# Summing neighbours' features: pass 1 quad by quad with ReLU ranks, and ten instead of eight destination blocks by row gathers

## The chip, the cores and the metric

The kernel runs on one core of a Trainium2 chip. In it PE (TensorE) does the matmuls, DVE (VectorE) the comparisons, sums and products, ACT (ScalarE) copies and the ReLU, POOL (GpSimd) issues the gathers, and SP (SyncE) issues ordinary transfers; SBUF is the on-chip memory, and PSUM the one that PE writes to. In the profiles an instruction is named by the tiles that it writes and reads (psa, pso and psg are tiles in PSUM). The metric is the device time of one execution in microseconds (us). Every time of a run is a median of several executions unless said otherwise, with the range where it matters. A profile is one further reading of such an execution: its span is the time from the first to the last recorded instruction.

The recorded comparison and six further jobs gave two kinds of times, and this document depends on keeping them apart. The same kernel before takes about 395 us on chips 12, 1 and 3 and about 483 us on chips 0, 2 and 13. I call them the **quick** and the **late** kind, and for short speak of quick and late chips. Each chip was met in one job only, so whether the kind belongs to the chip or to the occasion is not shown; within a job it never changed. The recorded comparison fell on the late kind. The state that each run carries ("fast", or "slow" when it is over 1.5% above the fastest of its kernel) compares runs of one job and doesn't show this. Where slow runs would shift a difference, the fast ones alone are taken, and the text says so.

## The reference

```python
def reference(node_features, edge_index_src, edge_index_dst):   # 4096 x 128 f32; 65536 edges
    output = np.zeros((num_nodes, dim), dtype=np.float32)
    for i in range(len(edge_index_src)):
        output[edge_index_dst[i]] += node_features[edge_index_src[i]]
    return output
```

## The kernel before

The 4096 destinations are 32 blocks of 128. Three parts matter.

**Pass 1** sorts edges by destination block. The edges lie in 24 chunks, handled as six quads of four; each edge needs its rank among the edges of its block, and then a one-hot of the rank moves it to its place by a matmul. Before, the ranks came from one-hots of the block number for half the edges at a time, running sums on DVE for the first half, running sums on PE for the second, and a product on DVE that picks each edge's own count.

**Gathered blocks.** For the first KG blocks, POOL fetches the source rows of 128 edges with one gather (three bf16 parts of x, 768 bytes a row), and PE adds them up with a one-hot of the destination. That is 24 gathers and 24 sums per block.

```python
    def gather(d, q):                                  # one unit: 4 gathers
        t = xg.tile([P, 4, 3 * P], BF16, name="rows", tag="xg")          # GB = 6 buffers
        for l in range(4):
            G.indirect_dma_start(out=t[:, l, :], out_offset=None, in_=x3d[:, :],
                in_offset=bass.IndirectOffsetOnAxis(ap=gidx[:, place(q).start + l, d:d + 1], axis=0))
        rows[d, q] = t
    def gather_sum(d, q):                              # one unit: 4 sums, rows -> psg
        oh = sb2.tile([P, 4, P], BF16, name="ohg", bufs=6)
        onehot(oh[:], gkey[:, place(q), d, :], 4)
        ...
        for l in range(4):
            PE.matmul(out=psg[d][:, :3 * P], lhsT=oh[:, l, :], rhs=t[:, l, :], ...)
```

**Dense blocks.** The others, in GROUPS, get a second ranking (pass 2), and then a slot each: PE makes the 4096x128 matrix of edge counts (`psa`, copied to `a` by ACT) and multiplies it with x (`pso`).

```python
    def blocks(k, oh, a):                              # 8 times per slot
        psa = ps.tile([P, 512], F32, name="psa", tag="psA", bufs=3)
        for i in range(4):
            PE.matmul(out=psa[:, i * P:(i + 1) * P], lhsT=oh[0][:, k*4+i, :], rhs=oh[1][:, k*4+i, :], ...)
        S.copy(out=a[:, k * 4:k * 4 + 4, :], in_=psa[:]...)
    def product(k, a, pso):
        for s in range(k * 4, k * 4 + 4):
            PE.matmul(out=pso[:, :3 * P], lhsT=a[:, s, :], rhs=x3[:, s, :, :]..., ...)
```

## Time and profile before

| | us |
|---|---|
| timed, recorded job (the 3 runs known to the prediction) | 485.02 (482.05 to 487.04) |
| span of the profile given | 395.4 |
| pass 1 ends (last move matmul) | 100.3 |
| first copy of a dense block | 141.2 |
| from there to the end of the last product | 243.9 |

### The profile page before, as it was taken

How to read it: one execution, taken by the hardware profiler on the slowest of the kernel's cores; microseconds unless marked ns; L12 is line 12 of the kernel's file. 1: busy time of each engine (PE TensorE's matmuls, PEld its weight loads, DVE VectorE, ACT ScalarE, POOL GpSimd, SP SyncE). 2: the span in 40 equal slices, each digit the busy share in tenths (PEclk: the TensorE clock that was granted, in tenths of full speed). 3: DMA queues.
4: the chain of work that ended last, by engine and by line, in shares of the span. 5: the costliest groups of instructions: out<-in, count | busy, mean ns of one | idle time of the engine just before them, and what ended most of it. 6: DMA issues, size and time to landing. Idle time of an engine off the chain costs nothing.

```text
span 395.4 us, 7887 instructions
## 1 busy us (share of the span) xinstructions
PE 315.8 (80%) x3274; PEld 229.8 (58%) x3274; DVE 303.5 (77%) x532; ACT 146.1 (37%) x271; POOL 226.8 (57%) x216
## 2 busy tenths in 40 slices
PE   0598765797544679676996999999979999999990
PEld 0255664775442567454674777676747776666650
DVE  4998899899899962838799797678898957676310
ACT  2485400100000044132543445455545455546520
POOL 5832038877812777733588777565785775673000
PEclk9999865676675698896998999999999999999995
DMA  8999732232200233321022333232332332332000
GB/s 245 188 162 158 219 120 70 61 81 70 56 17 12 59 82 81 95 57 48 26 57 76 76 86 87 68 80 69 83 78 68 87 92 68 86 87 66 8 14 10
DMA packets 31014, 32.14 MB, mean 81 GB/s; under 512 B 3904, under 2 KB 27648, under 8 KB 30976
## 3 DMA queue, kind: packets, MB, share of 16 engines
q0 software_dynamic: 17536, 23.08, 27.3%
q1 hardware_dynamic: 13296, 8.01, 7.0%
q8 instruction: 26, 0.43, 0.4%
q10 hardware_dynamic: 144, 0.52, 0.4%
q14 instruction: 12, 0.10, 0.1%
HBM read 22.02 MB, written 5.39 MB: 69 GB/s over the span
## 4 chain that ended last, share of the span: by engine, by line
PE 54%; DVE 39%; issue 3%; DMA 1%; ACT 1%; DVEq 0%
PE pso L495 29%; PE psa L489 10%; DVE p L258 9%; PE psg L313 7%; DVE oh L258 6%; DVE v L226 4%; PE ps L462 4%; DVE cum L430 3%; DVE oh L411 3%; DVE oh L153 3%; PE psr L239 2%; DVE cum L357 2%; PE psr L438 2%; DVE v L424 2%; DVE cum L236 2%
## 5 line engine op out<-in xcount | busy, mean ns | idle before, releaser
L299 POOL DMA_INDIRECT rows<-x3d,gidx x192 | 207.3, 1080 | 119.8 <-issue 71.4
L495 PE MATMUL pso<-x,a 128*128 128x384 bf16 x768 | 160.7, 335 | 0.1
L491 ACT CAST a<-psa 128x512 bf16<-128x512 f32 x192 | 111.7, 588 | 109.5 <-PE psa L489 108.6
L489 PE MATMUL psa<-oh 128*128 128x128 bf16 x768 | 76.1, 223 | 13.9 <-DVE oh L258 13.0
L495 PEld LDWEIGHTS <-a 128*128 128x128 bf16 x768 | 69.3, 100 | 28.0 <-issue 3.0
L489 PEld LDWEIGHTS <-oh 128*128 128x128 bf16 x768 | 59.9, 100 | 40.8 <-DVE oh L258 14.4
L258 DVE TENSOR_TENSOR oh<-psi,slo 128x4096 bf16<-128x4096 uint16 x24 | 54.7, 2278 | 0.0
L258 DVE TENSOR_TENSOR oh<-psi,dlo 128x4096 bf16<-128x4096 uint16 x24 | 54.7, 2277 | 0.0
L313 PE MATMUL psg<-rows,ohg 128*128 128x384 bf16 x192 | 41.2, 359 | 14.4 <-DVE ohg L258 13.1
L321 DVE TENSOR_REDUCE res<-pso 128x128 f32<-128x384 f32 x24 | 13.3, 553 | 40.5 <-PE pso L495 40.5
L271 PE MATMUL psm<-v,p 128*128 128x64 bf16 x512 | 34.1, 239 | 10.4 <-DVE p L258 8.8
L258 DVE TENSOR_TENSOR p<-psi,rank 128x2816 bf16<-128x2816 uint16 x24 | 37.5, 1614 | 3.7 <-ACT rank L243 3.7
L271 PEld LDWEIGHTS <-p 128*128 128x128 bf16 x512 | 30.8, 121 | 14.1 <-DVE p L258 13.3
L313 PEld LDWEIGHTS <-ohg 128*128 128x128 bf16 x192 | 19.2, 106 | 28.7 <-DVE ohg L258 14.0
L258 DVE TENSOR_TENSOR p2b<-psi,rank 128x768 bf16<-128x768 uint16 x48 | 23.3, 547 | 14.2 <-PE ps L462 7.4
L176 POOL DMA_DIRECT2D xf<-x x8 | 14.7, 2278 | 13.6 <-ACT x L174 12.2
L462 PEld LDWEIGHTS <-p2b 128*128 128x128 bf16 x576 | 20.0, 102 | 1.8 <-issue 0.3
L258 DVE TENSOR_TENSOR ohg<-psi,gkey 128x512 bf16<-128x512 uint16 x48 | 18.2, 412 | 0.0
L277 ACT CAST sa<-psm 128x128 bf16<-128x128 f32 x6 | 1.6, 266 | 43.4 <-PE psm L271 43.4
L462 PE MATMUL ps<-v,p2b 128*128 128x32 bf16 x480 | 16.9, 197 | 0.0
L174 ACT ACTIVATE x<-xf 128x1024 bf16<-128x1024 f32 x12 | 12.4, 1055 | 7.5 <-DMA xf<-in_node_features_dram 7.5
L411 DVE TENSOR_SCALAR oh<-sbk 128x96 bf16<-128x96 bf16 (+1 forms) x128 | 14.0, 209 | 1.3 <-ACT sbk L278 1.3
(78 smaller groups left out, 234.6 us busy)
## 6 DMA issues: line engine op xcount, KB each, us to landing
xf<-x POOLq DMA_DIRECT2D x8, 512.0 KB, 8.9
x3d<-x SPq DMA_DIRECT2D x4, 768.0 KB, 8.7
rows<-x3d,gidx POOLq DMA_INDIRECT x192, 2.9
xf<-in_node_features_dram SPq DMA_DIRECT2D x4, 512.0 KB, 7.5
out_dram<-res SPq DMA_DIRECT2D x32, 64.0 KB, 1.8
raw<-in_edge_index_src_dram ACTq DMA_DIRECT2D x1, 512.0 KB
raw<-in_edge_index_dst_dram SPq DMA_DIRECT2D x1, 512.0 KB, 5.1
x3d<-zrow SPq DMA_DIRECT2D x1, 96.0 KB, 5.7
```

The lines of the kernel that those rows point to most:

```text
L176: G.dma_start(out=xf[i][:], in_=part, accum_op=OP.add)
L226: V.tensor_tensor(out=v1[q][:, :, k], in0=oh1[q // QH][:, :, q % QH], in1=key[:, q, :, None, :].to_broadcast([P, NJ, NB, 4]), op=OP.mult)
L258: V.tensor_tensor(out=dst.rearrange("p i (m k) -> p i m k", k=2), in0=io.rearrange("p i (m k) -> p i m k", k=2), in1=keys2[:, :, None, :]. ...
L271: PE.matmul(out=psm[:, l * 64:(l + 1) * 64], lhsT=p1[:, l % 2, j, :], rhs=v1[q][:, j, :, :, l].rearrange("p k b -> p (k b)"), start=j == j ...
L299: G.indirect_dma_start(out=t[:, l, :], out_offset=None, in_=x3d[:, :], in_offset=bass.IndirectOffsetOnAxis(ap=gidx[:, place(q).start + l, ...
L313: PE.matmul(out=psg[d][:, :3 * P], lhsT=oh[:, l, :], rhs=t[:, l, :], start=q == 0 and l == 0, stop=q == NQ - 1 and l == 3)
L321: V.tensor_reduce(out=res[:], in_=pso[:, :3 * P].rearrange("p (v f) -> p f v", v=3), op=OP.add, axis=AX.X, negate=True)
L411: V.tensor_single_scalar(out=oh2[:, :, :, s, :], in_=sbk[:, :, ds].rearrange("p c (i k) -> p c i k", k=4), scalar=float(s + 1), op=OP.is_e ...
L462: PE.matmul(out=ps2[:, d % per * NB:(d % per + 1) * NB], lhsT=p2b[d % 2][:, c, :], rhs=v2[:, c, d // 4, :, d % 4], start=c == 0, stop=c == ...
L489: PE.matmul(out=psa[:, i * P:(i + 1) * P], lhsT=oh[0][:, s, :], rhs=oh[1][:, s, :], start=True, stop=True)
L491: S.copy(out=a[:, k * 4:k * 4 + 4, :], in_=psa[:].rearrange("p (s m) -> p s m", s=4))
L495: PE.matmul(out=pso[:, :3 * P], lhsT=a[:, s, :], rhs=x3[:, s, :, :].rearrange("p v f -> p (v f)"), start=s == 0, stop=s == NB - 1)
```

## The change

The intent: make pass 1 cheaper on DVE (six quads one after another, one wide one-hot each, ranks from PE and a ReLU that subtracts 4096 instead of a product), and take two of 24 dense slots off PE by gathering their rows instead. The core of the diff:

```diff
-KG = 8
-GROUPS = (4, 8, 8, 4)
+BIG = 4096.0
+KG = 10
+GROUPS = (4, 8, 8, 2)
...
-    def oh1s(h):
-        for b in range(NB):
-            V.tensor_single_scalar(... scalar=float(b), op=OP.is_equal)
+    def oh1s(q):
+        onehot(oh1q(q), kd[q][:], NL, NB)
+        for j in range(NJ):                      # column sums of each chunk quad
+            PE.matmul(out=pst[:, j:j + 1], lhsT=oh1q(q)[...], rhs=ones[:, :1], start=True, stop=True)
+    def scan(q):
+        V.tensor_tensor_scan(out=sums[q][:], data0=ones[:, :NJ], data1=pst[:, :NJ], ...)
...
-    for j in range(1, NJ):
-        V.tensor_tensor(out=c[:, j], in0=c[:, j - 1], in1=o[:, j - 1], op=OP.add)
-            V.tensor_tensor(out=cum1[h][:, js], in0=cum1[h][:, js], in1=oh1[h][:, js], op=OP.mult)
+    def counts(q):
+        for j0 in range(0, NJ, 4):
+            PE.matmul(out=psc[:, :n * P], lhsT=early[:], rhs=oh1q(q)[...], ...)   # adds BIG at own place
+            for j in range(max(j0, 1), j0 + n):
+                PE.matmul(out=psc[...], lhsT=sums[q][:, j - 1:j].to_broadcast([P, P]), rhs=identb[:], ...)
+            S.activation(out=cum[...], func=RELU, bias=minus[:], in_=psc[:, :n * P]...)
...
     def pass2(g):
-        g4 = gd // 4
+        kk = 4 if gd % 4 == 0 else 2             # lets the last group have two blocks
...
+    for q in range(NQ):
+        move1(q, during(q))                      # counts of quad q + 2 and parts of x in between
```

The x parts are now issued between the ReLUs; from the second group on nothing changes but the last group of two and the longer list of gathers.

## The prediction

> **What bounds the kernel now.** I read the engine shares first, then the chain that ended last, then the groups, and last the order-of-time view of single engines, because the shares alone hide that this program has three stages with different limits.
>
> ```profile
> PE 315.8 (80%) x3274; PEld 229.8 (58%) x3274; DVE 303.5 (77%) x532; ACT 146.1 (37%) x271; POOL 226.8 (57%) x216
> ...
> PE   0598765797544679676996999999979999999990
> ...
> POOL 5832038877812777733588777565785775673000
> PEclk9999865676675698896998999999999999999995
> ```
>
> PE looks like the bound and POOL like an engine with 43% to spare. The slices correct the second impression: POOL's work starts only in the sixth slice (one slice is 9.9 us) and stops at 361 us; in between it is at seven to eight tenths. PE is full only from about 190 us on.
>
> Stage one (0 to 100 us, keys and pass 1) belongs to DVE: in the chain of waits it is a row of DVE one-hots (p, 1.53 us each), spreads (v, two of 1.53), running sums (cum, 21 of 0.37) and products (cum, 2.3). Stage two (101 to 146 us) prepares the first dense group, DVE and PE by turns. Stage three is 24 dense slots, one destination block each, and belongs to PE:
>
> ```profile
> 379.88 5.21 PE pso L495 x32
> ```
> ```profile
> L299 POOL DMA_INDIRECT rows<-x3d,gidx x192 | 207.3, 1080 | 119.8 <-issue 71.4 <-PE psg L313 42.6 <-PE psa L489 4.3
> L495 PE MATMUL pso<-x,a 128*128 128x384 bf16 x768 | 160.7, 335 | 0.1
> ...
> L313 PE MATMUL psg<-rows,ohg 128*128 128x384 bf16 x192 | 41.2, 359 | 14.4 <-DVE ohg L258 13.1
> ```
>
> The first line is the chain's last long piece (start, length): the last dense product, with nothing to hide behind. The groups give busy time and mean, then the idle time before and its releaser. For the gathers (L299) "issue 71.4" matters: 0.30 us that POOL needs between two gathers, beside the 0.95 us of one. POOL waited for somebody else only 42.6 us, for buffers that PE had not yet summed. In order of time (start, length, idle before):
>
> ```profile
> 126.70 3.89 POOL L299 DMA_INDIRECT rows<-x3d,gidx  x1 [0.30 <-issue]
> 130.90 0.95 POOL L299 DMA_INDIRECT rows<-x3d,gidx  x1 [0.31 <-issue]
> 132.15 0.95 POOL L299 DMA_INDIRECT rows<-x3d,gidx  x1 [0.30 <-issue]
> ```
>
> So the gather rhythm is 1.248 us (130.90 to 132.15) even when nothing is in its way, and some gathers take up to 4.6 us: the one at 126.70 lies beside a DVE product of two SBUF operands that ran from 126.43 to 129.77. POOL's true occupation is 192 x 1.248 = 240 us, plus about 23 us of stretched gathers (the excess over 0.95 added up), plus 43 us of waits: 306 us, which is 55.5 to 361. **It is an engine with 43 us to spare, not 170.**
>
> **What the Trainium skill says.** "SBUF — State Buffer", section "Who interferes with whom": a DVE instruction with two SBUF inputs contends with a GpSimd instruction that reads SBUF, and the second to issue blocks fully. The trace agrees: the 3.89 us above, 4.58 at 200.6 (beside the spread of the third group), 4.08 at 214.6 (beside its product), while one-hots whose first operand lies in PSUM leave gathers at 0.95. "TensorE: Matmul & The Clock Gate", Part 1: an idle array drops to half clock and a sustained busy window of about 3.4 us restores it. The trace agrees: granted clock 0.50 to 0.8 in most 3 us windows of pass 1, 1.00 from 220 us. "ScalarE: Activation LUTs", section "What ACT_TABLE_LOAD costs": a pointer operand as bias adds about 93 ns; no run yet shows it here, it concerns the new ReLU. "Runtime: NRT & Kernel Launch", section "Model-switch cost" (some 70 us on the first execution after another program) with its launch sequence of some 15 us: I take from it, as an estimate, that the 89.6 us between the timed 485.02 and the span of 395.4 is a constant that both kernels pay. If it were proportional, the result would move by less than 2 us.
>
> **The change part by part.**
> Pass 1, DVE. Gone: 21 running sums (7.5 us), four products (9.2 us), 64 comparisons (10.9 us). New: six one-hots of 2816 elements, at the 1.53 us rhythm of p, 9.2 us; six scans and six key shifts of 0.2 to 0.3 us, about 3 us; four more fmax reductions, about 1 us. Kept: 12 spreads and 24 one-hots. DVE loses about 14 us of work. In addition the first quad need no longer wait for half the edges.
> Pass 1, PE and ACT. Per quad PE gets 22 one-column sums, six 512-column counts, 21 small additions and 32 rank matmuls; by 0.064 to 0.11 us each at half clock, and 0.43 for a wide one, that is about 8.5 us beside the 6.0 us of the move itself (88 at 0.069). ACT gets six ReLUs of 512 columns, 0.59 (the cast L491) plus the pointer's 0.09, so 4 us a quad. At half clock 14.5 us on PE exceeds DVE's 11 us a quad, at full clock it doesn't; and the scale parts of x now stand between the ReLUs on ACT and wait for accumulating transfers (8.9 us to landing). I follow it in order: first rank at 21 us (41 before), quads 0 and 1 held to about 49 us by those waits, then 10 to 11 us a quad: pass 1 ends at about 91 instead of 100, **9 us earlier**. Stage two keeps its work except for one unit of sums that moved forward: 2.4 us less. The dense stage starts about 11 us earlier.
> Dense stage, PE. A slot's core is eight steps of 0.874 us (four psa, four pso) = 7.0, plus 0.77 for its part of p2b. Two slots less: 15.5 us. Twelve units of four gathered sums more, 0.65 each: 7.8 us. Smaller last group: about 1 us. Net 8.7 less. **PE's own account is thus 11 + 9 = 20 us less**, to a span of about 376.
> POOL. 48 more gathers (240 instead of 192). When may it start? It needs the three-part copy of x in memory. Before: last part written by ACT at 44.7, first gather 55.5. After: the first scale part of the last quarter comes about 28 us in, then twice 9 us of accumulation and about 1.1 us of ACT, then the write: start at about 56 us, so hardly earlier. From there it is never short of buffers for long, since two to three sums a slot free them: 1.3 (first gather) + 240 x 1.248 = 299.5 + about 23 stretched (pass 1's products are gone, but the products of stage two, when POOL used to be idle, now meet gathers) + about 3 waits. Last gather issued at 383. Landing 1.7 more, the last sum and the last dense product 5.4, and the 10.3 us that today lie between the end of that product (385.1) and the end of the span: 400. **The path that ends last changes engine**: PE would be done near 376, POOL holds it to 400. With the constant 89.6 that is 489.8; I lower it by a little for the rivals and say 488.5.
>
> **The rivals.**
> A, PE stays the bound: 376 + 89.6 = 466. For it: PE is full for 180 us now, and someone who tunes would hardly have added a group size of two without a gain. Against it: 2.32 units a slot are 9.3 gathers or 11.6 us of POOL at the bare rhythm, against some 9.7 us of PE a slot; five units of lead at the start of the stage are used up after some 14 slots.
> B, the POOL bound holds, but without the stretching or with a start at 50: 384 to 390, timed 474 to 480. For it: the x parts are spread in time, so their transfers may land sooner. Against: the stretching operations of stage two are untouched.
> C, POOL bound and pass 1 worse than I think (ACT in order behind the accumulations, PE at half clock throughout): the gathers start at 62 or later, more waits, and the last product runs at half clock, 10 us instead of 5: span 408 to 412, timed 498 to 501.
> D, the timed executions run PE slower than the profiled one, and that makes the 90 us: then PE work removed counts more and the result is near 460. Against: nothing in the profile shows it.
>
> **Range and chances.** Main path 489.8, with 5 us for the start of the gathers, 6 for stretching and 4 for waits, about 8 in all if independent; A, B and D pull down, C up. Range 474 to 499. Faster than 475.3 needs nearly the whole of A or D: 0.17. Slower than 494.7 is the upper third of the main path plus C: 0.25. Within 2%: 0.58.
>
> **What would show it.** Right: POOL gathers back to back (0.30 us idle, "issue") from about 190 us to about 383; PE waiting for rows in psg (L314 or so) in the second half of the dense stage, some 15 to 30 us in all; the last 12 slots nearer 11.6 than 9.7 us; pass 1 over near 91, first gather near 56. Wrong: POOL still waiting for PE by tens of us and done 20 us before the end (then A), a median gather below 0.9 us, a first gather before 50 (B) or after 61 (C), or a difference between timed and profiled time that is not the same for both kernels (D).

## More of the kernel before

The page of the profile given of before has two more lines to keep. Columns of a group: engine, operation, output and input, count, busy us and mean ns, then the engine's idle us just before and who ended most of it. The chain line gives the share of each engine in the chain that ended last.

```profile
PE 54%; DVE 39%; issue 3%; DMA 1%; ACT 1%; DVEq 0%
...
L491 ACT CAST a<-psa 128x512 bf16<-128x512 f32 x192 | 111.7, 588 | 109.5 <-PE psa L489 108.6
```

PE and DVE together make 93% of the chain, and ACT's copies of psa wait for PE (108.6 of their 109.5 us of idle time).

## The result, and the profile after

| | before | after |
|---|---|---|
| recorded job, median (range, runs) | 483.53 us (477.55 to 487.04, 4) | 530.67 us (527.05 to 532.55, 4) |
| ratio of fast runs | | 1.1051, 95% interval 1.0918 to 1.1185 |

The change is **slower by 10.5%**, outside the predicted range. Ratios here and below are the mean time of one kernel's fast runs over that of the other's fast runs of the same rounds, so not quite the ratio of the medians quoted (here two of the four runs before, 485.02 and 487.04, lie over 1.5% above the fastest, 477.55, and the ratio fits the other two).

The profiled execution after took 527.05 us and its span is 525.4 us: a difference of 1.7, not 90. The page of the profile after, its lines on the span, the engines, the slices (tenths of 13.1 us each), the chain and three groups:

```profile
span 525.4 us, 8138 instructions
...
PE 331.8 (63%) x3395; PEld 226.5 (43%) x3399; DVE 276.3 (53%) x466; ACT 144.8 (28%) x274; POOL 265.4 (51%) x265
...
PE   2775642656250867669782588858568775784692
...
POOL 3350477256375225056886655546566546567300
PEclk9997875667655878789996888779788888899697
...
PE 40%; DVE 17%; another core or an unknown queue 16%; issue 16%; DMA 5%; ACT 3%; POOL 1%; SPq 0%; POOLq 0%; ACTq 0%
...
L300 POOL DMA_INDIRECT rows<-x3d,gidx x240 | 247.8, 1033 | 209.0 <-PE psg L314 98.6
...
L505 ACT CAST a<-psa 128x512 bf16<-128x512 f32 x176 | 98.3, 593 | 212.1 <-PE psa L503 84.5
```

No engine is full: PE 63%, POOL 51%, and the dense stage that stood at nine tenths on PE is now mostly at five to eight. POOL is not the bound here: it waits 98.6 us for PE to free its buffers. The chain names no engine for about a third of the span ("unknown queue" and "issue"). ACT's copies show where they wait for each other. The order of time of ACT and PE in a piece of the dense stage after (start us, length us, engine, instruction, and in brackets the idle time before and who ended it):

```profile
338.47 0.59 ACT L505 CAST a<-psa 128x512 bf16<-128x512 f32 x1 [0.23 <-PE psa L503]
...
338.92 0.39 PE L503 MATMUL psa<-oh 128*128 128x128 bf16 x4
...
339.79 0.39 PE L503 MATMUL psa<-oh 128*128 128x128 bf16 x4
...
340.67 0.39 PE L503 MATMUL psa<-oh 128*128 128x128 bf16 x4
...
341.29 0.59 ACT L505 CAST a<-psa 128x512 bf16<-128x512 f32 x1 [2.23 <-PE psa L503]
...
344.17 0.59 ACT L505 CAST a<-psa 128x512 bf16<-128x512 f32 x1 [2.30 <-remote]
...
344.81 0.38 PE L503 MATMUL psa<-oh 128*128 128x128 bf16 x4 [1.85 <-issue]
...
349.14 0.59 ACT L505 CAST a<-psa 128x512 bf16<-128x512 f32 x1 [4.38 <-issue]
349.77 0.58 PE L503 MATMUL psa<-oh 128*128 128x128 bf16 x4 [3.93 <-issue]
```

The four psa matmuls of 338.92 are over at 339.31, but ACT, idle since 339.06, starts their copy at 341.29. Those of 339.79 are copied at 344.17, those of 340.67 at 349.14. With three psa buffers PE runs ahead a little, then stands still for 1.85 and 3.93 us. The semaphore records of the same window say that ACT isn't what is late:

```
338.43 end of psa matmuls    338.45 PE's semaphore    338.47 ACT starts the copy
339.31 end of psa matmuls    341.27 PE's semaphore    341.29 ACT starts the copy
340.18 end of psa matmuls    344.15 PE's semaphore    344.17 ACT starts the copy
```

ACT starts 0.02 us after the record, as it should; the update comes 0.02 us after the matmul in the first row, 1.96 and 3.97 us after it in the others. For 49 of the 52 late copies of this profile the record is there, and ACT starts 0.02 us after each. (The ends of matmuls are modelled by the profiler; a delay of microseconds does not come from that, since the next matmuls have started meanwhile.) I call a copy **late** when it starts over 0.5 us after both its matmuls and the copy before it have ended. In the profile after 52 of 176 copies are late, and all lateness above 0.15 us sums to 136.9 us (this lets two copies overlap by 0.06 us; without it the sums here and in the table of runs are 1.4 to 2.8 us smaller on the late kind, and the counts the same). In the profile given of before it is 0 of 192, and 0.27 us. Was that the change, or the occasion?

Another thing separates the traces, and no run settles what it means. Of the 4,672 records of transfers' landings that the recorded kernel should leave (16 for each of its 240 gathers, and 832 others) 1,804 are there, and 1,676 of 3,904 in b_third; on the quick kind 4,563 of 4,672 (a_fourth), and with ordinary transfers in place of the gathers all 4,672 on a late chip too (a_poolplain). Lost records and late updates thus go together. Every timed run has a span and a granted clock, so each was traced: whether the updates would be late without tracing is not tested.

### The profile page after: what moved, and what is told of

Same layout as the page of the kernel before. It is cut to its first block, busy times and chain, and to the rows that moved or that the text cites. A ratio compares the mean times of both kernels' runs of the same rounds, so it can differ in the third digit from the quotient of the medians.

```text
span 525.4 us, 8138 instructions
## 1 busy us (share of the span) xinstructions
PE 331.8 (63%) x3395; PEld 226.5 (43%) x3399; DVE 276.3 (53%) x466; ACT 144.8 (28%) x274; POOL 265.4 (51%) x265
## 2 busy tenths in 40 slices
DMA packets 33320, 36.89 MB, mean 70 GB/s; under 512 B 4672, under 2 KB 29184, under 8 KB 33280
## 3 DMA queue, kind: packets, MB, share of 16 engines
q0 software_dynamic: 19840, 27.80, 24.0%
## 4 chain that ended last, share of the span: by engine, by line
PE 40%; DVE 17%; another core or an unknown queue 16%; issue 16%; DMA 5%; ACT 3%; POOL 1%; SPq 0%; POOLq 0%; ACTq 0%
PE pso L509 18%; PE psg L314 8%; PE psa L503 7%; DMA xf<-x 4%; DVE oh L190 4%; PE ps L476 2%; DVE p L190 2%; PE psm L274 2%; DVE oh L425 2%; ACT a L505 2%; DVE cum L444 2%; PE psr L452 1%; DMA xf<-in_node_features_dram 1%; DVE v L251 1%
## 5 line engine op out<-in xcount | busy, mean ns | idle before, releaser
L300 POOL DMA_INDIRECT rows<-x3d,gidx x240 | 247.8, 1033 | 209.0 <-PE psg L314 98.6
L505 ACT CAST a<-psa 128x512 bf16<-128x512 f32 x176 | 98.3, 593 | 212.1 <-PE psa L503 84.5
L314 PE MATMUL psg<-rows,ohg 128*128 128x384 bf16 x240 | 59.1, 401 | 38.4 <-DVE res L322 21.7
L314 PEld LDWEIGHTS <-ohg 128*128 128x128 bf16 x240 | 26.2, 115 | 61.3 <-issue 36.2
L274 PE MATMUL psm<-v,p 128*128 128x64 bf16 x512 | 26.7, 214 | 16.4 <-issue 10.6
L190 DVE TENSOR_TENSOR p<-psi,rank 128x2688 bf16<-128x2688 uint16 (+1 forms) x24 | 36.2, 1568 | 0.0
L190 DVE TENSOR_TENSOR p2b<-psi,rank 128x768 bf16<-128x768 uint16 x44 | 21.8, 550 | 22.7 <-remote 10.0
L274 PEld LDWEIGHTS <-p 128*128 128x128 bf16 x512 | 22.8, 112 | 21.0 <-issue 15.3
L230 ACT ACTIVATE cum<-psc,minus 128x512 bf16<-128x512 f32 (+1 forms) x36 | 21.9, 659 | 16.1 <-PE psc L227 6.5
L235 PE MATMUL psr<-cum,identb 128*128 128x88 bf16 x192 | 12.8, 226 | 20.5 <-issue 13.2
L235 PEld LDWEIGHTS <-identb 128*128 128x128 bf16 x192 | 10.6, 112 | 22.3 <-issue 22.3
```

The source lines that it names most:

```text
L190: V.tensor_tensor(out=dst.rearrange("p i (m k) -> p i m k", k=2), in0=io.rearrange("p i (m k) -> p i m k", k=2), in1=keys2[:, :, None, :]. ...
L230: S.activation(out=cum[:, :, 4 * j0:4 * (j0 + n)], func=RELU, bias=minus[:], in_=psc[:, :n * P].rearrange("p (t b) -> p b t", b=NB))
L235: PE.matmul(out=psr[:, :NL], lhsT=identb[:], rhs=cum[:, b, :], start=b == 0, stop=b == NB - 1)
L274: PE.matmul(out=psm[:, l * 64:(l + 1) * 64], lhsT=p1[:, l % 2, j, :], rhs=v1[q][:, 4 * j + l].rearrange("p k b -> p (k b)"), start=j == 0, ...
L505: S.copy(out=a[:, k * 4:k * 4 + 4, :], in_=psa[:].rearrange("p (s m) -> p s m", s=4))
```

## The experiments

Eighteen runs were made, in six jobs on six chips; each job also timed the kernel before on its own chip. "wrong" marks a kernel whose result is wrong on purpose; all others were correct. Medians are of all runs; two of the four were slow in a_kg8_again and in a_half_again (which is why no ratio was given), and their fast ones have 477.73 and 534.21 us in the mean.

| run | chip, kind | us, median | before there | ratio (95%) | span | copies late, sum us |
|---|---|---|---|---|---|---|
| b_same | 12 quick | 394.83 | 397.15 | 0.997 (0.989 to 1.006) | 391.2 | 0 of 192, 0.27 |
| b_kg10 | 12 quick | 419.91 | 397.15 | 1.055 (1.045 to 1.065) | 418.2 | 0 of 176, 0.27 |
| a_kg8 | 12 quick | 384.66 | 397.15 | 0.971 (0.964 to 0.978) | 382.3 | 0 of 192, 0.64 |
| a_same | 2 late | 530.49 | 483.13 | 1.102 (1.096 to 1.109) | 530.6 | 52 of 176, 135.6 |
| a_nogather, wrong | 2 late | 500.39 | 483.13 | 1.034 (1.022 to 1.047) | 497.6 | 34 of 176, 89.5 |
| a_kg8_again | 2 late | 483.08 | 483.13 | none given | 478.1 | 40 of 192, 81.4 |
| a_third | 0 late | 525.91 | 482.92 | 1.095 (1.085 to 1.104) | 524.2 | 51 of 176, 133.0 |
| a_gather0, wrong | 0 late | 367.57 | 482.92 | 0.765 (0.757 to 0.772) | 366.0 | 0 of 176, 0.27 |
| b_third, one look | 0 late | 481.74 | 482.92 | none | 480.0 | 42 of 192, 81.9 |
| a_fourth | 1 quick | 406.53 | 393.02 | 1.039 (1.031 to 1.046) | 404.0 | 0 of 176, 0.28 |
| a_half, wrong | 1 quick | 401.78 | 393.02 | 1.022 (1.017 to 1.027) | 400.1 | 0 of 176, 0.27 |
| a_plain, wrong | 1 quick | 367.60 | 393.02 | 0.935 (0.933 to 0.938) | 368.1 | 0 of 176, 0.27 |
| a_half_again, wrong | 13 late | 538.54 | 482.98 | none given | 533.6 | 44 of 176, 125.9 |
| a_plain_again, wrong | 13 late | 367.38 | 482.98 | 0.765 (0.756 to 0.773) | 365.7 | 0 of 176, 0.27 |
| a_poolplain, wrong | 13 late | 371.40 | 482.98 | 0.770 (0.765 to 0.776) | 369.6 | 0 of 176, 0.27 |
| a_kg4 | 3 quick | 408.85 | 395.89 | 1.039 (1.030 to 1.047) | 406.5 | 0 of 224, 1.6 |
| a_kg2 | 3 quick | 425.18 | 395.89 | 1.080 (1.069 to 1.090) | 423.0 | 0 of 240, 1.5 |
| a_kg8_third | 3 quick | 385.16 | 395.89 | 0.978 (0.970 to 0.986) | 383.7 | 0 of 192, 0.64 |

### First job: the two halves of the change apart

The theory was still the prediction's: pass 1 gains about 10 us, ten gathered blocks make POOL the bound. **b_same** is the kernel before once more; **b_kg10** has only the two further gathered blocks, **a_kg8** only the new pass 1.

```diff
 # b_kg10, against before (and kk = 4 or 2 in pass2, as in the change)
-KG = 8
-GROUPS = (4, 8, 8, 4)
+KG = 10
+GROUPS = (4, 8, 8, 2)
 # a_kg8, against after
-KG = 10
-GROUPS = (4, 8, 8, 2)
+KG = 8
+GROUPS = (4, 8, 8, 4)
```

> The kernel before, unchanged, profiled again beside its own timed runs. Open is why its timed runs take 482 to 487 us when the one profile of it has a span of 395.4, while the changed kernel's profile (525.4) and its times (527 to 533) agree. If there is a constant of about 88 us outside the span (my prediction's assumption), the new profile again shows about 395 beside times near 483. If the executions come in two kinds, one with late hand-overs between engines (in the changed kernel's trace the ACT copies of psa start up to 7.8 us after the matmul they wait for, 137 us in sum; in the profile of before at most 0.27 us late), the new profile's span is near 480 and shows copies that are late by 60 to 110 us in sum. Ratio 1.00 either way.

> The kernel before with only the second half of the change: 10 blocks by gathers and dense groups 4, 8, 8, 2. My recorded theory (POOL becomes the bound) expects 240 gathers at 1.25 us back to back and a time 10 to 20 us over before. The rival, that the late hand-overs come with the number of gathers and of their completions, expects most of the 47 us loss here: 510 to 530. If the loss comes from pass 1 alone: 475 to 490.

> The changed kernel with only the first half of the change: quad-by-quad pass 1, but 8 gathered blocks and dense groups 4, 8, 8, 4 as before. By my recorded account pass 1 ends 9 us earlier and stage two is 2 us shorter, so 470 to 478. If the loss lies in pass 1 or in how the new order hands work between engines, 510 to 530.

This chip was of the quick kind: before took 397.15 us, near its span, instead of 485. Ten gathered blocks cost 22.8 us (419.91 less 397.15), the new pass 1 gains 12.5 us (397.15 less 384.66). The second is close to the prediction's 11 us; the first is a little over the 10 to 20 that I expected. The forecasts in absolute times, for a chip on which before takes 485, met no such chip here, and b_same left its question open. The page of b_kg10, with POOL's slices and two groups:

```profile
POOL 5732058777508777775877777777777777777700
...
L299 POOL DMA_INDIRECT rows<-x3d,gidx x240 | 251.7, 1049 | 111.2 <-issue 84.0
...
L313 PE MATMUL psg<-rows,ohg 128*128 128x384 bf16 x240 | 54.9, 360 | 36.1 <-DMA rows<-x3d,gidx 19.4
```

From about 200 us POOL is at seven tenths or more to the end, 0.30 us of issue for every 0.95 us of gather being the rest, and PE now waits for rows: 19.4 us ended by a gather's landing, where before had only waits for DVE. And for pass 1, the chain in order of time, of a_kg8 and then of the profile given of before (start, length, what):

```profile
90.25 0.91 DVE fmax L397 x6
91.15 6.85 DVE oh L425 x64
```
```profile
100.79 7.01 DVE oh L411 x64
```

Stage two's first work, the one-hots of the first dense group, starts 9.6 us earlier.

### Second job: a late chip

**a_same** is the change unchanged. **a_nogather** leaves out the gathers of the two added blocks, 48 of 240, and lets PE sum parts of x that already lie in SBUF; all other work stays.

```diff
     def gather(d, q):
         t = xg.tile([P, 4, 3 * P], BF16, name="rows", tag="xg")
+        if d >= 8:
+            rows[d, q] = x3[:, q * 4:q * 4 + 4].rearrange("p s v f -> p s (v f)")
+            return
```

> The changed kernel, unchanged, in another session. In the session of the first three runs the kernel before took 397 us and no ACT copy of psa was over 0.4 us late; pass 1 alone gave -12.5 us (384.7), ten gathered blocks alone +22.8 (419.9). If POOL is the bound in such a session, as my record says, the two halves do not add up freely: POOL's 240 gathers set the end, about 400 us in the profile, 398 to 410 timed, within 3% of before. If the late hand-overs of the recorded profile belong to the changed kernel itself and not to the session, this is 520 to 535 again.

> Wrong results on purpose for two destination blocks: the changed kernel, but for blocks 8 and 9 nothing is gathered, and their 48 sums read rows of x that already lie in SBUF. PE keeps all 240 sums and the 22 dense slots, POOL has 192 gathers. If the gathers of POOL hold the end (recorded theory), 370 to 380: PE's own account of the record. If the added sums on PE or the smaller last group cost the time, it stays within 3 us of the changed kernel.

> The changed kernel with 8 gathered blocks once more, on the same chip as the two above. In a session without late hand-overs 383 to 387; in one with them it shows whether the first half of the change still gains there: before near 483, this one 3% less, 465 to 475, if the delays fall on all kernels alike; more than before if the added hand-overs between PE, ACT and DVE of the new pass 1 pay them.

Here the change is again at 530 us and before at 483. So the 10.5% is repeatable, on this kind of chip. Without the 48 gathers it is 500.39, neither of the two outcomes expected; by the medians of fast runs (530.49 - 499.27) / 48 = 0.65 us per gather, and the sum of late copies falls from 135.6 to 89.5. POOL's rhythm can't explain that, since POOL in this kind stands waiting for PE. And a_kg8, 12.5 us faster than before on the quick chip, is within 1% of it here (fast runs 477.7 against 481.6 in the mean): most of the gain of pass 1 disappears as well.

### Third job: no gathers at all

**a_gather0** has the same edit with `d >= 0`: no gathers, the same number of sums, slots and copies. **a_third** and **b_third** are the two kernels as controls.

> The changed kernel once more, unchanged. Two kinds of occasions have shown up: one in which the kernel before takes 397 us and no hand-over from PE to ACT is late, one in which it takes 483 us and copies of psa start up to 7.8 us late, 80 us in sum with 192 gathers in the quad-by-quad kernel and 136 us with 240. On an occasion of the quick kind: 398 to 410, as the two halves and my record say (POOL bound). On one of the late kind: 527 to 533.

> Wrong results on purpose: the changed kernel without any gather; all 240 sums read rows of x that lie in SBUF. In the traces of the late kind every late copy (52 of 176 in the changed kernel) had a gather issued within the 4 us before its release, and none of the copies without one was late. If the gathers cause the late hand-overs, this kernel has none even on an occasion of the late kind and takes 365 to 380 on either kind. If the delay belongs to the chip or to the occasion as such, it takes 440 or more on one of the late kind.

> The kernel before, one look. On an occasion of the late kind its trace should show, for the first time, what its 483 us consist of: copies of psa late by about 80 us in sum, about 0.4 us for each of its 192 gathers as in the quad-by-quad kernel with as many. On one of the quick kind it repeats 391 to 396 with none late.

Another late chip (before 482.92). Without gathers the changed kernel takes 367.57 us, and no copy is late:

```profile
span 366.0 us, 7833 instructions
...
L508 ACT CAST a<-psa 128x512 bf16<-128x512 f32 x176 | 102.3, 589 | 105.9 <-PE psa L506 105.9
```

So (525.91 - 367.57) / 240 = 0.66 us per gather, near the 0.65 of the second job from another chip and another number of gathers. Two rivals fall: a slow clock of the chip and slow copies would have been there without gathers too. The granted clock is lower in late profiles with gathers (0.78 to 0.84, against 0.86 to 0.90 in quick ones), but a_gather0 ran at 0.925 on a late chip: so the low clock comes with the gathers and not with the chip. That it follows from PE's waiting is likely and not shown.

b_third gives what had been missing: a profile of the kernel before on a late chip. Its page:

```profile
span 480.0 us, 7887 instructions
...
L299 POOL DMA_INDIRECT rows<-x3d,gidx x192 | 203.7, 1061 | 205.9 <-PE psg L313 126.0
...
L491 ACT CAST a<-psa 128x512 bf16<-128x512 f32 x192 | 108.4, 591 | 160.8 <-PE psa L489 104.8
```

The span is 480.0, not 395.4. The copies' mean is 591 ns (588 before), POOL's busy time is no more, but ACT's idle time has grown by 51 us and POOL waits 126 us for PE. The late hand-overs are in the kernel before as well; the profile given had simply been taken on an occasion of the quick kind.

### Fourth and fifth job: which property of a gather

Two readings were left for what makes a hand-over late: any transfer of so many rows that lands meanwhile, or only a gather; and if the gather, its rows or its number. **a_fourth** is the change unchanged, **a_half** gathers 64 rows instead of 128, **a_plain** replaces each gather by an ordinary transfer of 128 rows from the sync engine's queue, **a_poolplain** issues those from POOL.

```diff
 # a_half
-                out=t[:, l, :], ... ap=gidx[:, place(q).start + l, d:d + 1]
+                out=t[:64, l, :], ... ap=gidx[:64, place(q).start + l, d:d + 1]
-            PE.matmul(... lhsT=oh[:, l, :], rhs=t[:, l, :], ...)
+            PE.matmul(... lhsT=oh[:64, l, :], rhs=t[:64, l, :], ...)
 # a_plain (a_poolplain: G.dma_start)
-            G.indirect_dma_start(out=t[:, l, :], ...)
+            at = ROW0 + (4 * q + l) * P
+            nc.sync.dma_start(out=t[:, l, :], in_=x3d[at:at + P, :])
```

> The changed kernel unchanged, as the control of the two runs beside it. If the chip is of the late kind (kernel before near 483): 525 to 533 us again, with about 50 of 176 copies of psa over 0.5 us late, about 135 us in all. If it is of the quick kind (kernel before near 397): no late copies, POOL bound, about 400 to 412 us, that is 1% to 4% slower than the kernel before there. Rival: the change is slower by some 10% on a quick chip as well; then the late hand-overs are not the cause of the 10%.

> The changed kernel with every gather fetching 64 rows instead of 128 (the sums contract 64 partitions; the result is wrong on purpose); the number of gathers stays 240. On a late chip: if lateness comes per gather (its issue, its completion), copies stay as late as in the control, sum about 135 us, time 520 to 531. If it comes per row fetched, the sum halves to about 68 us and the time falls to about 455 to 470. On a quick chip it only tells whether a gather's 0.95 us depends on its rows.

> The changed kernel with each of its 240 gathers replaced by an ordinary transfer of 128 rows of the same 768 bytes each from the same memory into the same buffers, from the sync engine's queue (wrong result on purpose). On a late chip: if any transfer that lands in SBUF meanwhile makes the hand-overs late, it stays near the control, 500 to 530 us. If it takes a gather issued by POOL, no copy is late and the time is that of the run without gathers, 366 to 378 us. On a quick chip 366 to 378 in both cases.

The chip of the fourth job was quick, so a_half and a_plain said little about lateness there (and ran again in the fifth), but a_fourth is what the prediction had described: **the change on a quick chip takes 406.53 us, 3.9% slower than before**. Its page and, in order of time, the end of its chain:

```profile
POOL 4155017778887777778787777777777777777700
...
L300 POOL DMA_INDIRECT rows<-x3d,gidx x240 | 252.2, 1051 | 94.4 <-issue 64.9
...
L314 PE MATMUL psg<-rows,ohg 128*128 128x384 bf16 x240 | 53.3, 352 | 39.7 <-DMA rows<-x3d,gidx 21.8
```
```profile
379.11 0.95 POOL rows L300
380.36 0.95 POOL rows L300
381.61 0.95 POOL rows L300
382.87 2.94 DMA rows<-x3d,gidx
386.33 7.73 PE pso L509 x32
```

Gathers back to back, the last at 382.87 (the count said 383), its landing, then the last product: POOL holds the end. Against a_plain, with the same PE work and no gathers, the gathers cost 406.53 - 367.60 = 39 us on this kind. a_half shows that a gather's length hardly depends on its rows (group means 997 and 1051 ns) and so gains only 5 us.

> 240 gathers of 64 rows instead of 128 (wrong result on purpose); the time of the kernel before tells the kind of chip. On a late chip (before near 483): lateness per gather would leave the time at 515 to 531 with about 135 us of late copies; lateness per row fetched would give about 68 us of it and 455 to 470. On a quick chip: 402 again, with none late.

> 240 ordinary transfers of 128 rows of 768 bytes from the sync engine's queue instead of the gathers (wrong result on purpose). On a late chip: 480 to 530 with tens of late copies if any transfer of so many rows does it, 366 to 378 with none late if it takes the gather engine. On a quick chip: 367 again.

> The same 240 ordinary transfers, issued by the gather engine POOL instead of the sync engine (wrong result on purpose). On a late chip: if the indirect addressing does it, none late and 366 to 385; if anything that POOL's own queue writes and completes does it, tens of late copies and 470 to 530. On a quick chip it tells POOL's cost of a direct transfer beside the 0.95 us of a gather: at the same 1.25 us rhythm about 400, else less.

The fifth job met a late chip, where the same kernels decide. a_half_again has half the rows and stays at 535.2 and 533.3 us in its two fast runs (541.9 and 548.5 were slow), with 125.9 us of late copies, where the whole gathers had 133.0 to 136.9: **the lateness goes with the number of gathers, hardly with their rows**. And neither kind of ordinary transfer of as many rows and bytes makes any copy late. From POOL's own queue, the page of a_poolplain:

```profile
L301 POOL DMA_DIRECT2D rows<-x3d x240 | 131.5, 557 | 169.6 <-PE psg L312 149.4
L503 ACT CAST a<-psa 128x512 bf16<-128x512 f32 x176 | 102.3, 589 | 106.1 <-PE psa L501 106.1
```

Set the second line against the one of after: idle time 106.1 us instead of 212.1, all of it ended by PE. 371.40 us, against 534.2 for the fast runs of a_half_again in the same job. So it isn't POOL's queue, nor the volume: that queue carries 19,840 packets and 27.80 MB in a_poolplain as in the change. Nor is it the number of completions: the Trainium skill, "DMA: Bandwidth & Descriptors", section "Why a DMA increments its semaphore by 16 and not by 1", says that a transfer issued by GpSimd posts all 16 increments whatever its shape, so these 240 complete with as many as the gathers do. The trace of a_poolplain agrees (4,672 landing records, 832 + 240 x 16); for the gathers, whose records are partly missing, no run shows it. What is left is the gather instruction itself, or the scattered addresses that it reads. What in it, and why only on some chips, no run here shows.

### Sixth job: fewer gathers in a correct kernel

```diff
-KG = 10
-GROUPS = (4, 8, 8, 2)
+KG = 4                        # a_kg2: KG = 2
+GROUPS = (4, 8, 8, 8)         # a_kg2: (4, 8, 8, 8, 2)
```

> The changed kernel with 4 gathered blocks (96 gathers) and a last dense group of eight (28 slots); correct result. Worked out from the 385 us of eight gathered blocks on a quick chip: four slots of 7.77 us more, 24 units of sums of 0.65 us less, so about 400 us on a quick chip (a few us slower than before's 395). On a late chip, at (483 minus 385) / 192 = 0.51 us per gather, 96 x 0.51 = 49 more: about 449, some 7% faster than the kernel before. Rival: the lateness doesn't depend on the number of gathers once there are any, then about 480 to 500.

> The same with 2 gathered blocks (48 gathers) and dense groups of 4, 8, 8, 8 and 2 (30 slots); correct result. Quick chip about 408 us. Late chip 408 + 48 x 0.51 = 432, some 10% faster than the kernel before. Rival as above: 480 or more.

> The new pass 1 with 8 gathered blocks as before (192 gathers), beside the other two. Quick chip 384 to 386, the fastest of the three; late chip 476 to 488, the slowest of the three and level with the kernel before.

The chip was quick, so the question for the late kind stays open. On the quick kind four blocks cost 408.85 and two 425.18, some 9 and 17 us more than I had worked out; a dense slot that replaces a gathered block costs (425.18 - 385.16) / 6 = 6.7 us net, not the 3.9 that I had put (7.77 less six sums of 0.65). With ten at 406.53 on another quick chip, **eight gathered blocks are the best of the four numbers that ran** (2, 4, 8 and 10), and a_kg8 is the best correct version: 2.2 and 2.9% faster than before on two quick chips, within 1% of it on a late one, and there 10% faster than the change (fast runs 477.73 against 530.98 in the mean). For a late chip my estimate, from 0.485 us per gather (the 93.1 us between a_kg8's fast runs on the two kinds over 192 gathers, taken as proportional), is 408.85 + 96 x 0.485 = 455 for four blocks and 448 for two, both ahead of before's 483; it has not been run.

## Why the prediction was wrong

The stages, read from the start and end of their instructions in each trace, show it at once (us):

| kernel, kind | pass 1 ends | first dense copy | from there to the end of the last product | span |
|---|---|---|---|---|
| before, quick (profile given) | 100.3 | 141.2 | 243.9 | 395.4 |
| after, quick (a_fourth) | 90.1 | 129.3 | 264.7 | 404.0 |
| before, late (b_third) | 114.2 | 178.2 | 291.4 | 480.0 |
| after, late (recorded) | 120.1 | 175.0 | 340.4 | 525.4 |
| after without gathers, late (a_gather0) | 91.4 | 130.6 | 230.3 | 366.0 |

**The step that failed** is the one on the two times of before: "that the 89.6 us between the timed 485.02 and the span of 395.4 is a constant that both kernels pay". There is no such constant. In every run whose time and span are of the same execution they differ by about 1.7 us (527.05 and 525.4; 481.74 and 480.0; 405.61 and 404.0). So does the profile given: its own entry says that this execution took 397.01 us, against the span of 395.4. The page that the prediction drew on for its constant, the Trainium skill's "Runtime: NRT & Kernel Launch", section "Model-switch cost", says itself that steady-state calls skip this cost, and these times repeat; the page was not wrong, its use was. The 89.6 us lay between two occasions, and on the late one they are hand-overs that come late while gathers are in flight, some 0.65 us of time per gather. They come with the gathers, which the change raises from 192 to 240. In the dense stage the kernel before issues 132 of them in 24 slots (b_third, 5.5 a slot), the one after 180 in 22 (8.2 a slot). By the table, the dense stage of before loses 291.4 - 243.9 = 47.5 us on the late kind against the quick one; that of after loses 340.4 - 230.3 = 110.1 against its own run without gathers. That is 62.6 us more, less the 13.6 us by which that run is shorter than before's quick one (243.9 - 230.3): 49.0 us longer. With 3.2 us gained before the stage and 0.4 after it, this is the whole 45.4 us between the two late spans. The two baselines are not of one kind, since before without gathers was not run. Each against its own quick run, the losses are 47.5 and 75.7 us (340.4 - 264.7), or 0.36 and 0.42 us a gather of the stage. So the greater number is shown, and a dearer gather where they are denser only hinted at. a_nogather points the same way, being some 20 us slower in its fast runs than a_kg8_again with as many gathers and two slots fewer, but it also has 48 more sums, and its own quick time is not known. Why density should count is only argued: with three psa buffers PE can run through a short lateness, as in the window shown, but not through one after another.

**Pass 1** was right where nothing is late: "pass 1 ends at about 91 instead of 100" was measured as 89.0 to 91.8 in every quick profile; timed gain 12.5 and 10.7 us (chips 12 and 3), put at about 11. On the late kind its end moves from 114.2 to 120.1 instead: against a_gather0's 91.4 it loses 29 us, where before loses 14 (114.2 less 100.3), and that eats the gain. That it has more hand-overs from engine to engine after the first gather, near 58 us, is the likely reason and was not tested. "The dense stage starts about 11 us earlier" measured 11.9 on the quick kind and 3.2 on the late one.

**PE's own account**, "to a span of about 376": without gathers it is 365.7 to 368.1 when no transfer comes from POOL. The direction was right, and the term was undersized by 8 to 10 us. In a_gather0 they stand in two places: the dense stage is 13.6 us shorter and not 8.7, and from the last product to the end it takes 5.1 us instead of the 10.3 that the sum kept. What makes these two differ was not looked into.

**POOL becomes the bound**: right on the quick kind, step by step. Start "at about 56": 58.5. "Last gather issued at 383": 382.9. PE waiting for rows "some 15 to 30 us": 21.8, 19.5 of it after 260 us. The last 12 slots "nearer 11.6 than 9.7 us": 11.6 from one last product's end to the next. Span 400: 404.0; of the 4 us, the last rows landed 2.94 us after their issue instead of 1.7, and the last product took 7.73 us at a granted clock of 0.68, where in the profile given it took 5.21 at 1.00. That the last gather came out within 0.1 us has some luck in it: the start was 2.5 us late, and the waits counted as 3 us were 0.2. The predicted difference between the spans, 4.6 us, was 8.6 (404.0 less 395.4), and between the times on one chip 13.5 (406.53 less 393.02), since the times of before itself run from 391.7 to 398.7 us on the quick kind. On the late kind the bound doesn't form: POOL waits 98.6 us for PE and issues its last gather at 493.2, 32 us before the end. That is the sign that the prediction named for its rival A, and A was wrong all the same: PE wasn't full but waiting.

**The rivals.** A (PE stays the bound, 466) and B (POOL without stretching) fell on both kinds. C named a late start of the gathers and more waits with 498 to 501; the waits came, not by its cause. D, that the timed executions differ from the profiled one, was true of the occasion. But it expected more PE time in them, so that less PE work would pay more and the result be near 460; what they have more of is waiting per gather, and it went the other way. I had left it with "nothing in the profile shows it", which was correct and no argument, because the profile was of another kind than the times.

**The chances**: 0.25 for slower was too little, and the range of some 2.5% to either side rested on the offset being constant, which no term of its width covered. On a quick chip too the answer is slower (3.9%), by the mechanism described; adding a constant of 90 us to both sides had shrunk that as well, to under 1%.

## What to carry to other kernels

If a profile's span and the timed runs of the same kernel differ by more than a few us, they are of different occasions: compare the profile with the time of its own execution first (397.01 for the span of 395.4 here), and get a profile of the slower occasion before predicting from either, as one run of b_third would have done. Work out an exchange such as gathers for matmuls for both, since the cheap side on one (0.16 us of time per gather on a quick chip, 39 us over 240) can cost four times as much on the other (0.66). And look at the delay between the end of an instruction and the start of the one that it releases, not at engines' shares alone: no engine was over 63% busy here, and 52 hand-overs from PE to ACT were over 0.5 us late.

## What the Trainium skill lacked or had wrong

- No page has it: in three of six jobs, each on a chip of its own, the records of PE's semaphore updates come late while gathers are issued, and ACT's copies start up to 7.8 us late (52 of 176 over 0.5 us; 0 of 176 without gathers); 0.65 to 0.66 us of time per gather, and the same kernel at 483 instead of 395 us. It belongs to "DMA: Bandwidth & Descriptors", beside "SWDGE vs HWDGE vs iDMA". That section explains how transfers issued by GpSimd can be held up by DVE through the descriptor rings in SBUF; of an effect in the other direction, on the updates of other engines, it says nothing, and 240 ordinary transfers from the same engine left all copies on time.
- No page has the rhythm of a gather on POOL: 0.95 us and 0.30 us of issue, nearly the same for 64 rows (mean 997 ns) as for 128 (1051 ns); an ordinary transfer issued by POOL took 0.56 us on average.
- "ScalarE: Activation LUTs", section "What ACT_TABLE_LOAD costs": the ReLU of 512 columns with a pointer bias took 694 ns (30 of them, a_fourth), the plain cast of 512 columns 589: 105 ns more, where the page states about 93 for a pointer operand. The two are not the same instruction otherwise, so this is no test of the page.
